# One product of 512 columns for the two that share a weight's high part, in the last swiglu of a two-layer hybrid block

## The chip, the core and the metric

The kernel runs on one core of one Trainium2 chip. The metric is the device time of one execution in microseconds; the profiled execution also has a span, from its first to its last instruction. The engines are TensorE (PE; PEld is its weight load), VectorE (DVE), ScalarE (ACT), GpSimd (POOL) and SyncE (SP, which issues the DMAs).

## The reference

256 tokens of x and 256 of a context, 1024 features wide, go through two layers. Each layer is a swiglu, a mixer (a short convolution in the first, attention in the second) and another swiglu, each behind an RMS norm that is modulated by a condition. The context is dropped after the attention, so the last swiglu works on 256 tokens alone:

```python
def _swiglu(h, w13, w2):
    gte, up = jnp.split(h @ w13, 2, axis=-1)
    return (jax.nn.silu(gte) * up) @ w2
...
lat = lat + 0.5 * mod[:, 2, 2] * _swiglu(_modulate(lat, norm_g[i, 2], mod[:, 2, 0], mod[:, 2, 1]), ffn_w13[i, 1], ffn_w2[i, 1])
```

w13 is 1024 x 5632 (gate and up, 2816 each), w2 is 2816 x 1024, all in float32.

## The kernel before

Features lie on the 128 partitions, tokens in the columns: x is a tile of 8 feature blocks (KT = 8) x 512 columns (S = 256 tokens of x, then 256 of the context; T2 = 512).

**Three matmuls per product.** Every float32 operand is split into a high part that TensorE's fp32r format holds and the low part that is left (`split`, L97: ACT writes the high part, L98, and DVE subtracts it from the source, L99). A product of a weight w and a moving operand m is then wh*mh + wh*ml + wl*mh, three matmuls into the same PSUM region: `mm3`, L122 to L124. The weight is the stationary operand (128 x 128), and each matmul loads its own.

**The last swiglu** is `ffn(1, 1, hn, S, ...)` at the end of the kernel, with tot = S = 256 columns. Its 22 blocks of 128 hidden features are done in three parts ("thirds") of 8, 7 and 7:

- *Gate part.* For each block, `load_w` fetches 1 MB of w13 over SP's queue and splits it in two halves of 1024 columns (up first, then gate; four buffers for the halves of each part). `w13_mm` runs over the 8 k of the input features and, for each, makes the gate product into PSUM tile pg and the up product into pu. `w13_post` applies Silu (ACT, L535, to sg), multiplies by up (DVE, L537, to gm) and splits the result into gh and gl, two tiles of a pool with 8 buffers each.
- *Second product* (`project`). For each of 8 output tiles m, w2's weights are split (896 or 1024 columns), products over the third's 7 or 8 blocks go into PSUM tile py, and `finish` (L453, DVE) adds gate * py to x. The first two output tiles are begun with all blocks but the last, then both get the last block; the other tiles follow one by one. In the last third, each finished tile goes out with a DMA (L1143).

The input h of this swiglu is made by `norm_k` for each k: DVE scales x (t, L264), ACT adds the bias and writes the high part hh (L274), DVE writes the low part hl (L275). They lie in tiles of class `Plain`: with w = S each tile of 1024 columns holds the high, or the low, parts of four k.

PSUM has six buffers of 512 columns for pg, pu and py. The order of instructions on each engine is made by a planner that goes by estimated times and priorities; only the start of the kernel has PE's order written out by hand.

The output projection of the attention ahead of it (`by_pairs("wo")`) also calls `project` with 256 columns, with operands in two separate slices (aos).

Of the kernel before, what the change touches and what calls it, by code (L numbers as in the profile page):

```python
# [16 lines left out]
P = 128  # L17
# [24 lines left out]
def hybrid_kernel(ctx: ExitStack, tc: tile.TileContext, a: dict, out: bass.AP):  # L42
# [54 lines left out]
    def split(hi, lo, src):  # L97
        nc.scalar.activation(out=hi, in_=src, func=AF.Copy)  # L98
        nc.vector.tensor_tensor(out=lo, in0=src, in1=hi.bitcast(F32), op=ALU.subtract)  # L99
# [17 lines left out]

    def mm3(ps, w, m, first, last, more=False):
        wh, wl = w
        mh, ml = m  # L120
        kw = {"skip_group_check": True} if more else {}
        nc.tensor.matmul(ps, wh, mh, start=first, stop=False, **kw)  # L122
        nc.tensor.matmul(ps, wh, ml, start=False, stop=False, **kw)  # L123
        nc.tensor.matmul(ps, wl, mh, start=False, stop=last, **kw)  # L124
# [155 lines left out]
    def hot(s, dt=F32R):  # L280
        return hop.tile([P, 1024], dt, name=nm(s), tag="hop")

    class Plain:


        def __init__(self, w=T2):
            self.w, self.n = w, 1024 // w
            self.t = [(hot("hh"), hot("hl")) for _ in range(KT // self.n)]

        def at(self, k, c0, c1):  # L290
            o = (k % self.n) * self.w
            return tuple(t[:, o + c0 : o + c1] for t in self.t[k // self.n])

    def pick(h, k, c0, c1):
        return h.at(k, c0, c1)
# [92 lines left out]
    def new_pair(s):  # L388

        return (  # L390
            gp.tile([P, T2], F32R, name=nm(s + "h"), tag="gh"),
            gp.tile([P, T2], F32R, name=nm(s + "l"), tag="gl"),
        )
# [51 lines left out]

        return tail

    def finish(m, ps, c0, c1, gate, tail):
        g = gate()
        for s in range(2):  # L450
            if c0 <= s * S < c1:
                o = s * S - c0
                nc.vector.scalar_tensor_tensor(  # L453
                    out=x[:, m, s * S : s * S + S],
                    in0=ps[:, o : o + S],
                    scalar=g[:, m, s : s + 1],
                    in1=x[:, m, s * S : s * S + S],
                    op0=ALU.mult,
                    op1=ALU.add,
                )  # L460
        if tail:
            tail(m, c0, c1)
# [6 lines left out]
    def project(ws, src, nk, gate, tail, tot, late, ev, between=()):  # L469

        def products(ps, w, ks, c0, c1):
            for k in ks:
                mm3(ps[:, : c1 - c0], w(k), src(k, c0, c1), k == 0, k == nk - 1)

        nf = 3 if between else 2  # L480
        ahead = {}

        def get(m):
            for i in range(m, min(m + 3, KT)):
                if i not in ahead:
                    ahead[i] = ws(i)
            return ahead[m]

        w2 = [get(m) for m in range(nf)]
        p2 = [psum("py") for _ in range(nf)]  # L490
        cut = nk - 2 if between else nk - 1
        for i in range(nf):
            products(p2[i], w2[i], range(cut), 0, tot)
            if i < len(between):
                between[i]()
        if between:
            for i in range(nf):
                products(p2[i], w2[i], (nk - 2,), 0, tot)
        for i in range(nf):
            products(p2[i], w2[i], (nk - 1,), 0, tot)  # L500
            finish(i, p2[i], 0, tot, gate, tail)
            tick(ev)

        for m in range(nf, KT - late):
            if tail and tot == S and m == KT - 2:
                ready()
            w = get(m)
            ps = psum("py")
            products(ps, w, range(nk), 0, tot)
            finish(m, ps, 0, tot, gate, tail)  # L510
            tick(ev)
        if late:

            wl = [get(m) for m in (6, 7)]
            if tail:
                ready()
            for s in range(2):
                for i in range(2):
                    ps = psum("py")
                    products(ps, wl[i], range(nk // 2), s * S, s * S + S)  # L520
                    flush(1)
                    products(ps, wl[i], range(nk // 2, nk), s * S, s * S + S)
                    finish(6 + i, ps, s * S, s * S + S, gate, tail)


    def w13_mm(pp, w, h, ks, c0, c1):
        for k in ks:
            mv = pick(h, k, c0, c1)
            for i in range(2):
                mm3(pp[i][:, c0:c1], w((1 - i) * 1024 + k * P), mv, k == 0, k == KT - 1)  # L530

    def w13_post(pp, g, c0, c1):
        n = c1 - c0
        sg = tp.tile([P, T2], F32, name=nm("sg"), tag="sg", bufs=3)
        nc.scalar.activation(out=sg[:, :n], in_=pp[0][:, :n], func=AF.Silu)  # L535
        gm = tp.tile([P, T2], F32, name=nm("gm"), tag="gm", bufs=3)
        nc.vector.tensor_tensor(out=gm[:, :n], in0=sg[:, :n], in1=pp[1][:, :n], op=ALU.mult)  # L537
        split(g[0][:, c0:c1], g[1][:, c0:c1], gm[:, :n])

    class Pair:  # L540

# [76 lines left out]
    def ffn(l, b, h, tot, gate, tail, gs=(), ev=1.5):  # L618
        gs = list(gs)
        i0 = 0  # L620
        for t, n in enumerate(THIRDS):
            between = ()
            if tot == T2:
                heads = []
                if t == 0 and not gs:

                    w = [load_w(a["w13"][l, b, 0])]
                    gs = [new_pair("g") for _ in range(2)]
                    pp = [(psum("pg"), psum("pu")) for _ in range(2)]
                    w13_mm(pp[0], w[0], h, range(KT), 0, S)  # L630
                    flush()
                    w.append(load_w(a["w13"][l, b, 1]))
                    w13_mm(pp[1], w[1], h, range(KT), 0, S)
                    h.sums(0)
                    w13_mm(pp[0], w[0], h, range(KT), S, T2)
                    w13_post(pp[0], gs[0], 0, T2)
                    heads.append(Pair(a["w13"][l, b, 2], h))
                    h.sums(1)
                    heads[0].sums(0)
                    w13_mm(pp[1], w[1], h, range(KT), S, T2)  # L640
                    w13_post(pp[1], gs[1], 0, T2)
                    heads[0].head()
                    h.sums(2)
                    heads[0].sums(1)
                prev = None
                for i in range(len(gs), n):
                    if t == 0 and not heads and i in AS_IS[l, b]:
                        w = load_w(a["w13"][l, b, i])
                        pp = psum("pg"), psum("pu")
                        if prev:  # L650
                            prev.seven()
                        w13_mm(pp, w, h, range(4), 0, T2)
                        if prev:
                            gs.append(new_pair("g"))
                            prev.four(gs[-1])
                            prev = None
                        w13_mm(pp, w, h, range(4, KT), 0, T2)
                        gs.append(new_pair("g"))
                        w13_post(pp, gs[-1], 0, T2)
                        tick(5)  # L660
                        continue
                    if heads:
                        pr = heads.pop(0)
                    else:
                        pr = Pair(a["w13"][l, b, i0 + i], h)
                        pr.sums(0)
                        pr.sums(1)
                        pr.head()
                    pr.five()
                    if prev:  # L670
                        prev.seven()
                    pr.six()
                    if prev:
                        gs.append(new_pair("g"))
                        prev.four(gs[-1])
                    prev = pr

                def last():
                    gs.append(new_pair("g"))
                    prev.four(gs[-1])  # L680

                between = (prev.seven, last) if prev else ()
            else:
                for i in range(n):
                    w = load_w(a["w13"][l, b, i0 + i])
                    gs.append(new_pair("g"))
                    pp = psum("pg"), psum("pu")
                    w13_mm(pp, w, h, range(KT), 0, tot)
                    w13_post(pp, gs[i], 0, tot)
                    tick(1)  # L690
            i0 += n
            box = {}
# [1 line left out]
            def ws2(m):  # L694
# [9 lines left out]
            cur = gs  # L704
            end = t == len(THIRDS) - 1
            project(
                ws2, lambda k, c0, c1: (cur[k][0][:, c0:c1], cur[k][1][:, c0:c1]), n,
                gate, tail if end else None, tot, 2 if end and tot == T2 else 0, ev, between,
            )
            gs = []  # L710
# [423 lines left out]
    mix(HEADS - 1, pts.pop(HEADS - 1))  # L1134


    hn = Plain(S)
    project(
        by_pairs("wo"), lambda k, c0, c1: aos[k], KT, lazy_gate(1, 1), tail_norm(1, 2, hn), S, 0, 0,
    )  # L1140
# [84 lines left out]
```

## Time and profile before

| | us |
|---|---|
| median of three runs | 1597.02 (1593.21 to 1598.21) |
| the profiled execution | 1595.53 |
| its span | 1593.7 |
| of that, the last swiglu: first matmul to last | 1398.37 to 1590.21 |
| gate part of its thirds (8, 7, 7 blocks) | 47.8, 40.2, 40.2 |
| second product of its thirds | 22.9, 20.0, 20.0 |
| mean granted TensorE clock | 0.993 |

The parts of the thirds are given from the start of their first matmul to the start of their last. In the last swiglu TensorE runs 22 x 16 x 3 = 1056 matmuls for the gate part and 22 x 8 x 3 = 528 for the second product, all of 256 columns.

How to read the lines: a row of the timeline gives start, length, engine, line of the kernel, operation, output <- inputs and shapes, a count if several were merged, and in brackets the idle time before it and what ended it. The length of a matmul holds its way through the array and overlaps with the next one; the distance of two starts is what one costs in a row.

### The profile page before, as it was taken

The numbers are of one execution on the slowest core, as the hardware profiler recorded it, in microseconds if no ns is written. First come the engines' busy times: TensorE is split into PE (matmuls) and PEld (weight loads), VectorE is DVE, ScalarE is ACT, GpSimd is POOL, SyncE is SP. The second block draws the span as 40 slices with busy tenths as digits, with TensorE's granted clock in tenths as the row PEclk, the third lists the DMA queues.
The fourth block names the chain that finished last, engine by engine and source line by source line (L and its number), as shares of the span: only waits on it lengthen the run. The fifth ranks groups of instructions, "written<-read, shape, count | busy, mean of one in ns | idle before, by whom it ended". The sixth has DMA issues, their size and how long they took to land.

```text
span 1593.7 us, 25820 instructions
## 1 busy us (share of the span) xinstructions
PE 1568.8 (98%) x10666; PEld 1449.7 (91%) x10666; DVE 1303.3 (82%) x1984; ACT 721.1 (45%) x1103; POOL 29.4 (2%) x20
## 2 busy tenths in 40 slices
PE   8999999999999999999999999999999998899999
PEld 7688998999888899989899899899899897899999
DVE  5998888979999879798798879898797789876554
ACT  6522452544322356335345365335255455644443
POOL 0000000000000000000000000000000005200000
PEclk9999999999999999999999999999999999999999
DMA  9465324334565522452342513443433554556452
GB/s 359 181 238 207 110 99 153 133 102 176 177 219 195 175 68 93 148 170 100 129 156 96 180 56 107 158 136 99 169 118 120 208 186 151 200 185 220 166 200 102
DMA packets 39575, 248.79 MB, mean 156 GB/s; under 512 B 5409, under 2 KB 7201, under 8 KB 14625
## 3 DMA queue, kind: packets, MB, share of 16 engines
q1 hardware_dynamic: 36864, 245.38, 43.9%
q10 hardware_dynamic: 2592, 1.76, 0.4%
q8 instruction: 83, 1.36, 0.3%
q14 instruction: 36, 0.29, 0.1%
HBM read 244.77 MB, written 1.05 MB: 154 GB/s over the span
## 4 chain that ended last, share of the span: by engine, by line
PE 92%; DVE 4%; ACT 2%; DMA 1%; issue 0%; POOL 0%; ACTq 0%; DVEq 0%; POOLq 0%
PE py L123 10%; PE py L122 10%; PE py L124 10%; PE p L124 7%; PE p L123 7%; PE p L122 6%; PE q L122 5%; PE q L124 5%; PE q L123 5%; PE pg L122 2%; PE pg L124 2%; PE pg L123 2%; PE pu L124 2%; PE pu L123 2%; PE pu L122 2%; PE pv L122 1%
## 5 line engine op out<-in xcount | busy, mean ns | idle before, releaser
L98 ACT ACTIVATE wh<-wr 128x1024 fp32r<-128x1024 f32 (+2 forms) x276 | 276.4, 1014 | 388.0 <-PE py L123 140.7
L99 DVE TENSOR_TENSOR wl<-wr,wh 128x1024 fp32r<-128x1024 f32 (+2 forms) x276 | 319.9, 1166 | 88.2 <-ACT wh L98 87.9
L142 DVE CUSTOM_DVE_ANT_0 junk<-wr,scbc,modb 128x1024 bf16<-128x1024 f32 x224 | 286.9, 1281 | 31.8 <-DMA wr<-in_modT 29.0
L122 PE MATMUL py<-gh,wh 128*128 128x512 f32 (+1 forms) x746 | 263.3, 353 | 0.0
L123 PE MATMUL py<-gl,wh 128*128 128x512 f32 (+1 forms) x746 | 263.0, 353 | 0.0
L124 PE MATMUL py<-gh,wl 128*128 128x512 f32 (+1 forms) x746 | 262.7, 352 | 0.0
L99 DVE TENSOR_TENSOR wl<-ws,wh 128x1024 fp32r<-128x1024 f32 x108 | 131.6, 1223 | 34.1 <-ACT wh L98 34.0
L124 PEld LDWEIGHTS py<-gh,wl 128*128 128x128 f32 x746 | 141.1, 189 | 19.0
L122 PEld LDWEIGHTS py<-gh,wh 128*128 128x128 f32 x746 | 141.2, 189 | 18.6
L123 PEld LDWEIGHTS py<-gl,wh 128*128 128x128 f32 x746 | 141.2, 189 | 18.1
L98 ACT ACTIVATE wh<-ws 128x1024 fp32r<-128x1024 f32 x108 | 113.9, 1058 | 71.3 <-PE p L123 44.5
L124 PE MATMUL p<-th,wl 128*128 128x256 f32 x432 | 122.3, 283 | 0.0
L123 PE MATMUL p<-tl,wh 128*128 128x256 f32 x432 | 122.2, 283 | 0.0
L122 PE MATMUL p<-th,wh 128*128 128x256 f32 x432 | 122.2, 283 | 0.0
L453 DVE SCALAR_TENSOR_TENSOR x<-py,G,x 128x256 f32<-128x256 f32 x168 | 73.9, 477 | 23.1 <-PE py L124 23.1
L122 PE MATMUL q<-bh,wh 128*128 128x256 f32 x320 | 90.6, 283 | 0.0
L123 PE MATMUL q<-bl,wh 128*128 128x256 f32 x320 | 90.6, 283 | 0.0
L124 PE MATMUL q<-bh,wl 128*128 128x256 f32 x320 | 90.6, 283 | 0.0
L122 PEld LDWEIGHTS p<-th,wh 128*128 128x128 f32 x432 | 82.9, 192 | 0.3
L123 PEld LDWEIGHTS p<-tl,wh 128*128 128x128 f32 x432 | 82.9, 192 | 0.3
L124 PEld LDWEIGHTS p<-th,wl 128*128 128x128 f32 x432 | 82.9, 192 | 0.0
L124 PE MATMUL pg<-hh,wl 128*128 128x256 f32 (+1 forms) x240 | 75.5, 315 | 2.8 <-DVE wl L99 2.7
(236 smaller groups left out, 4045.2 us busy)
## 6 DMA issues: line engine op xcount, KB each, us to landing
wr<-in_w SPq DMA_DIRECT2D x88, 1024.0 KB, 4.9
wr<-in_modT SPq DMA_DIRECT2D x64, 1024.0 KB, 5.0
wr<-in_w2b SPq DMA_DIRECT2D x32, 896.0 KB, 4.6
wr<-in_w2a SPq DMA_DIRECT2D x16, 1024.0 KB, 4.9
pm<-in_mod SPq DMA_DIRECT2D x16, 512.0 KB, 10.0
wr<-in_cw_cx SPq DMA_DIRECT2D x8, 1024.0 KB, 4.9
wr<-in_cw_b SPq DMA_DIRECT2D x4, 1024.0 KB, 5.0
wr<-in_cw_out SPq DMA_DIRECT2D x4, 1024.0 KB, 4.9
```

The source lines that it names most:

```text
L98: nc.scalar.activation(out=hi, in_=src, func=AF.Copy)
L99: nc.vector.tensor_tensor(out=lo, in0=src, in1=hi.bitcast(F32), op=ALU.subtract)
L122: nc.tensor.matmul(ps, wh, mh, start=first, stop=False, **kw)
L123: nc.tensor.matmul(ps, wh, ml, start=False, stop=False, **kw)
L124: nc.tensor.matmul(ps, wl, mh, start=False, stop=last, **kw)
L142: nc.vector.tensor_tensor_reduce(out=junk, in0=raw[:, j * D : j * D + D], in1=scbc[:, v, :], scale=1.0, scalar=modb[:, l, col : col + 1], ...
L453: nc.vector.scalar_tensor_tensor(out=x[:, m, s * S : s * S + S], in0=ps[:, o : o + S], scalar=g[:, m, s : s + 1], in1=x[:, m, s * S : s * ...
```

## The change

In the last swiglu the high and low part of an operand now lie side by side in one tile. `Beside` holds h that way (two k per tile, each 256 columns high and 256 low), and one tile gx of 512 columns takes the place of gh and gl. An operand that comes as three views (high, low, both) is multiplied with two matmuls: the weight's high part meets both in one of 512 columns, and the weight's low part meets the high part in one of 256 columns, into the first half of the PSUM tile. So the PSUM tile holds wh*mh + wl*mh in the first half and wh*ml in the second, and the halves are added when they are read.

For gate and up this is `beside_post`: ACT copies the second half out of PSUM, DVE adds the first to it, for both, and Silu, product and split follow as before on 256 columns. In the second product `finish` adds gate * half to x once for each half. The last output tile (m = 7) of each third keeps the three matmuls of 256 columns.

```diff
     def mm3(ps, w, m, first, last, more=False):
         wh, wl = w
+        kw = {"skip_group_check": True} if more else {}
+        if len(m) == 3:
+
+            nc.tensor.matmul(ps, wh, m[2], start=first, stop=False, **kw)
+            nc.tensor.matmul(ps[:, :S], wl, m[0], start=False, stop=last, **kw)
+            return
         mh, ml = m
-        kw = {"skip_group_check": True} if more else {}
...
+    class Beside:
+
+
+        def __init__(self):
+            self.t = [hot("hx") for _ in range(KT // 2)]
+
+        def both(self, k):
+            o = (k % 2) * T2
+            return beside(self.t[k // 2][:, o : o + T2])
+
+        def at(self, k, c0, c1):
+            return self.both(k)[:2]
+
+    def beside(t):
+        return t[:, :S], t[:, S:], t
...
-    def finish(m, ps, c0, c1, gate, tail):
+    def finish(m, ps, c0, c1, gate, tail, wide=False):
         g = gate()
         for s in range(2):
-            if c0 <= s * S < c1:
-                o = s * S - c0
+            for o in [s * S - c0] if not wide else range(0, T2 if s == 0 else 0, S):
+                if not c0 <= s * S < c1:
+                    continue
                 nc.vector.scalar_tensor_tensor(
...
-        def products(ps, w, ks, c0, c1):
+        def products(ps, w, ks, c0, c1, wide=True):
             for k in ks:
-                mm3(ps[:, : c1 - c0], w(k), src(k, c0, c1), k == 0, k == nk - 1)
+                m = src(k, c0, c1)
+                if not wide:
+                    m = m[:2]
+                n = T2 if len(m) == 3 else c1 - c0
+                mm3(ps[:, :n], w(k), m, k == 0, k == nk - 1)
...
-            products(ps, w, range(nk), 0, tot)
-            finish(m, ps, 0, tot, gate, tail)
+            wide = len(src(0, 0, tot)) == 3 and m < KT - 1
+            products(ps, w, range(nk), 0, tot, wide)
+            finish(m, ps, 0, tot, gate, tail, wide)
...
+    def beside_post(pp, g):
+
+        sg = tp.tile([P, T2], F32, name=nm("sg"), tag="sg", bufs=3)
+        gm = tp.tile([P, T2], F32, name=nm("gm"), tag="gm", bufs=3)
+        for o, p in ((sg, pp[0]), (gm, pp[1])):
+            nc.scalar.copy(o[:, S:], p[:, S:])
+            nc.vector.tensor_tensor(out=o[:, :S], in0=p[:, :S], in1=o[:, S:], op=ALU.add)
+        nc.scalar.activation(out=sg[:, :S], in_=sg[:, :S], func=AF.Silu)
+        nc.vector.tensor_tensor(out=gm[:, :S], in0=sg[:, :S], in1=gm[:, :S], op=ALU.mult)
+        split(g[0], g[1], gm[:, :S])
...
-                    gs.append(new_pair("g"))
+                    gs.append(beside(gp.tile([P, T2], F32R, name=nm("gx"), tag="gh")))
                     pp = psum("pg"), psum("pu")
-                    w13_mm(pp, w, h, range(KT), 0, tot)
-                    w13_post(pp, gs[i], 0, tot)
+                    for k in range(KT):
+                        for j in range(2):
+                            mm3(pp[j], w((1 - j) * 1024 + k * P), h.both(k), k == 0, k == KT - 1)
+                    beside_post(pp, gs[i])
...
-    hn = Plain(S)
+    hn = Beside()
```

More of the change, by code (lines that the diff above doesn't have):

```diff
@@ L283, in hybrid_kernel, with __init__ @@
     class Plain:
-        def __init__(self, w=T2):
-            self.w, self.n = w, 1024 // w
-            self.t = [(hot("hh"), hot("hl")) for _ in range(KT // self.n)]
+        def __init__(self):
+            self.t = [(hot("hh"), hot("hl")) for _ in range(KT // 2)]
         def at(self, k, c0, c1):
-            o = (k % self.n) * self.w
-            return tuple(t[:, o + c0 : o + c1] for t in self.t[k // self.n])
+            o = (k % 2) * T2
+            return tuple(t[:, o + c0 : o + c1] for t in self.t[k // 2])
+    class Beside:
+        def __init__(self):
+            self.t = [hot("hx") for _ in range(KT // 2)]
+        def both(self, k):
+            o = (k % 2) * T2
+            return beside(self.t[k // 2][:, o : o + T2])
[3 more added lines that the diff above has]
+        return t[:, :S], t[:, S:], t
     def pick(h, k, c0, c1):
@@ L500, in project @@
             products(p2[i], w2[i], (nk - 1,), 0, tot)
-            finish(i, p2[i], 0, tot, gate, tail)
+            finish(i, p2[i], 0, tot, gate, tail, len(src(0, 0, tot)) == 3)
             tick(ev)
@@ L706, in ffn @@
             project(
-                ws2, lambda k, c0, c1: (cur[k][0][:, c0:c1], cur[k][1][:, c0:c1]), n,
+                ws2,
+                (lambda k, c0, c1: cur[k]) if tot == S
+                else lambda k, c0, c1: (cur[k][0][:, c0:c1], cur[k][1][:, c0:c1]), n,
                 gate, tail if end else None, tot, 2 if end and tot == T2 else 0, ev, between,
```

## The prediction

> **What bounds the kernel now.** I read the page first (busy time by engine, chain that ended last), then the windows of the last swiglu, then its matmuls in order of time, then the places where work on other engines could come on the path.
>
> ```profile
> PE 1568.8 (98%) x10666; PEld 1449.7 (91%) x10666; DVE 1303.3 (82%) x1984; ACT 721.1 (45%) x1103; POOL 29.4 (2%) x20
> ...
> PE 92%; DVE 4%; ACT 2%; DMA 1%; issue 0%; POOL 0%; ACTq 0%; DVEq 0%; POOLq 0%
> ```
>
> TensorE is busy all the time, and 92% of the chain is its matmuls. The windows cut the last swiglu into gate part and second product of each third (columns: window, its length, busy time and instructions of PE, PEld, DVE, ACT, POOL, clock, DMA share, GB/s):
>
> ```profile
> 1398.30:1446.30 48.00, 47.92 (x384) 47.72 (x385) 32.85 (x53) 23.39 (x38) 0.00 (x0) 0.96 0.61 218
> 1446.30:1469.30 23.00, 23.00 (x194) 23.00 (x193) 14.72 (x18) 9.81 (x11) 0.00 (x0) 1.00 0.60 204
> 1469.30:1509.60 40.30, 40.30 (x338) 40.30 (x338) 19.61 (x26) 17.17 (x26) 0.00 (x0) 1.00 0.48 164
> 1509.60:1529.80 20.20, 20.20 (x171) 20.20 (x170) 13.92 (x18) 9.23 (x11) 0.00 (x0) 1.00 0.61 205
> ```
>
> No window has a hole in PE; DVE is at 49 to 69%, ACT at 43 to 49%, DMA at about 0.6. So a matmul saved here is time saved, as long as nothing else becomes late. The second gate part is 7 tiles x 48 = 336 matmuls of 256 columns; the first starts at 1469.38 and the last at 1509.58, 335 pitches in 40.20 us: **0.1200 us** each. Where 512 columns are used (conv stage, first start 411.10, last 557.31, 645 pitches) it is **0.2267 us**. One product of 512 is cheaper than two of 256: 0.2400 - 0.2267 = 0.0133 us. A mix of both lengths stands in the second layer's first swiglu (start, length, engine, line):
>
> ```profile
> 1239.37 0.39 PE L124 MATMUL py<-gh,wl 128*128 128x512 f32 x1
> 1239.60 0.28 PE L122 MATMUL p<-th,w4h 128*128 128x256 f32 x1
> 1239.71 0.28 PE L123 MATMUL p<-tl,w4h 128*128 128x256 f32 x1
> ...
> 1240.91 0.28 PE L124 MATMUL p<-th,w4l 128*128 128x256 f32 x1
> 1241.03 0.40 PE L122 MATMUL py<-gh,wh 128*128 128x512 f32 x1
> 1241.26 0.40 PE L123 MATMUL py<-gl,wh 128*128 128x512 f32 x1
> ```
>
> A 256 after a 512 starts 0.23 us later, a 512 after a 256 starts 0.12 us later: the pitch belongs to the matmul that runs, and a change of length costs nothing.
>
> **The change, part by part.**
>
> *Merged products.* Gate part: 22 tiles x 8 k x 2 (gate, up) = 352 products. Second product: 22 k x 7 output tiles = 154; the eighth tile (m = 7) keeps three matmuls in every third. Each of the 506 goes from 3 x 0.1200 = 0.3600 to 0.2267 + 0.1200 = 0.3467 us: 506 x 0.0133 = **-6.73**. In the first 3.4 us of the stage (1398.37 to 1401.8) the 256 columns have a pitch of 0.213, which is 256 columns at half of the rate and no fixed part; some 5 products there save nothing: **+0.07**. The output projection keeps its three matmuls.
>
> The Trainium skill, "TensorE: Matmul & The Clock Gate", section "Back-to-back issue gap", puts the fixed part of a warm matmul at 2.5 ns beside N/2.4. By it a merge would be worth 2.5 ns and all 506 about 1.3 us, an estimate from that page. The trace says 13.3 ns, at 256 and at 512 columns alike, and the sum goes by the trace.
>
> *Start of the stage.* The wide product needs both parts of h, the first product of before only the high one.
>
> ```profile
> 1397.81 0.91 ACT L274 ACTIVATE hh<-t,mod 128x256 fp32r<-128x256 f32 x2 [2.13 <-DVE t L264]
> 1398.37 0.58 PE L122 MATMUL pg<-hh,wh 128*128 128x256 f32 x1 [1.11 <-ACT hh L274]
> 1398.47 0.48 DVE L275 SCALAR_TENSOR_TENSOR hl<-t,mod,hh 128x256 fp32r<-128x256 f32 x1
> ```
>
> PE starts 0.06 after the first hh; it will start 0.04 or so after the first hl, at 1398.99: **+0.62**. Later k are not late: the hl come at 0.42 each, a k costs PE 2 x (0.427 + 0.213) = 1.28 us while slow (512 columns at twice 0.213) and 2 x 0.3467 = 0.69 after, and the last two hl (ready 1404.45 and 1404.88) meet PE at about 1404.7.
>
> *Longer way from gate product to g.* For each of 22 tiles: two copies on ACT (0.36 each, row L602 of 256 columns out of PSUM) and two adds on DVE (0.41, as gm of L537; 0.36 between starts) come ahead of Silu. Inside a third nothing waits for g. What could wait is the next weights: DVE's second split of a tile ends at 1501.73 (start 1500.51, 1.22 long) and its matmuls start at 1503.84, 2.11 us to spare. A tile then lasts 5.55 in place of 5.74, and two adds take 0.72: 1.20 us are left, so 0. At the end of a third the second product needs the last g:
>
> ```profile
> 1569.94 0.95 ACT L98 ACTIVATE wh<-wr 128x896 fp32r<-128x896 f32 x1 [2.90 <-PE pg L123]
> 1570.80 0.37 ACT L535 ACTIVATE sg<-pg 128x256 f32<-128x256 f32 x1
> ...
> 1572.39 0.42 ACT L98 ACTIVATE gh<-gm 128x256 fp32r<-128x256 f32 x1 [0.38 <-DVE gm L537]
> ```
>
> ```profile
> 1570.93 1.09 DVE L99 TENSOR_TENSOR wl<-wr,wh 128x896 fp32r<-128x896 f32 x1 [3.00 <-ACT wh L98]
> 1571.94 0.41 DVE L537 TENSOR_TENSOR gm<-sg,pu 128x256 f32<-128x256 f32 x1
> 1572.27 1.09 DVE L99 TENSOR_TENSOR wl<-wr,wh 128x896 fp32r<-128x896 f32 x1
> 1573.27 0.42 DVE L99 TENSOR_TENSOR gl<-gm,gh 128x256 fp32r<-128x256 f32 x1
> ```
>
> PE begins the second product at 1570.17 and covers 2 output tiles x 6 k before it needs the last g: 2 x 6 x 0.36 = 4.32, to 1574.49; gl ends at 1573.69. Afterwards the cover is 4.16. Walking the queues with the same splits in them (wl, add, add, wl, then gm, gh, gl, since gm waits for Silu while wl is ready) gl ends about 4.8 after the start: 0.65 late. In the third with 8 tiles the cover is 14 x 0.3467 = 4.85 against about 5.05: 0.2 late. Together 0.65 + 0.65 + 0.2 = 1.5. With gm ahead of the second split, or with PE given products of the third output tile meanwhile, it is 0. The upper bound is all new work in series, 2 copies 0.72 + 2 adds 0.82 + Silu behind them 0.47 + gh no longer under a split 0.5 = 2.5: late by 1.9, 1.9 and 1.5, 5.3 in all. Between 0 and the walk I take **+0.75**.
>
> *finish.* 21 more x += gate * ps on DVE. A pair takes 0.88 where one takes 0.48 (row L453 x2 at 1575.06); in the second product DVE then works 1.09 + 0.88 = 1.97 of 2.43 us per tile, and the second one lies under the 0.95 of ACT's next weight split, which the DVE split awaits anyway: 0. Uncovered it would be 21 x 0.40 = 8.4. The last tile is as before, so the tail after the last matmul (0.48 and the output) is too.
>
> *Storage.* hx takes four buffers as hh and hl did, gx one where there were two; no DMA is added or moved, and a weight MB per 5.55 us asks for 4% more than now, at a share of 0.6. 0.
>
> **Sum:** -6.73 + 0.07 + 0.62 + 0.75 = **-5.29 us**. The profiled execution took 1595.53 (span 1593.7 and 1.8 around it): **1590.2**. Against the median 1597.02 of the three runs it would be 1591.7; those runs spread over 5 us, and the profiled one lies inside them. 0.3% of the time is 4.8 us.
>
> **Rivals.**
>
> *The g chain stalls every third.* For it: only 0.8 us are spare now, and two engines with strict order take part. Against it: PE can be given other products. With the upper bound 5.3 in place of 0.75: 1595.53 - 6.04 + 5.3 = 1594.8, no measurable change.
>
> *The fixed part isn't saved.* If the cost went by columns alone, nothing is gained and 0.62 + 0.75 is paid: 1596.9. Against it stands 0.2267 in place of 0.24 in every stage with 512 columns, and the mix above. If a part of it is saved, the time lies between 1596.9 and 1590.2. By the page of the Trainium skill named above it would be about 1595.6, with 2.5 ns a product; the trace speaks against it.
>
> *Slower: DVE holds the weights back.* If its order puts the whole chain of a tile (two copies and adds 2 x 0.77, Silu 0.37, gm 0.41, gh 0.42, gl 0.42: 3.2 us) ahead of the second weight split, that split comes 2.9 later than now (0.24 lies between the two splits today), against 1.92 to spare. PE then waits 1.0 us in each of the 19 tiles that another gate tile follows in its third: 1590.2 + 19 = 1609. It decides from 1.92 us of delay on, and is slower than before from 0.5 us per tile. For it: DVE and ACT already take turns on each tile. Against it: a ready split is let ahead of gm in every tile of the trace (wl, gm, wl, gl).
>
> *It doesn't do what it says* where a product falls back to three matmuls; by the code only m = 7 does, and that is in the sum.
>
> **How the numbers follow.** Forecast 0.64, its own range 1588 to 1592.5 (stalls of 0 to 2, and some 1 us of run to run); as its middle is just over the bound of 4.8, 0.54 of it is faster by over 0.3% and 0.10 within. Stalled thirds 0.16 and no fixed part, or a small one, 0.10: both within 0.3%. DVE holding weights back 0.10: slower. So faster 0.54, same 0.36, slower 0.10. The range goes from 1587.5 (no stall, a run 1 us under this one) to 1596.0, which takes in the stalled thirds and the small fixed part.
>
> **What would show it.** Matmuls from 10666 to 10160; in the last swiglu pitches of 0.227 and 0.120 in turn, a gate tile in 5.55 us and an output tile in 2.43 (2.77 in the first third); the first matmul of the stage about 0.6 us later, behind hl; PE idle of under 1 us at the three starts of the second product, put down to the split of g. It is wrong if a 256 after a 512 of the same bank has another pitch, if weight splits show up ahead of idle PE in every tile, or if the work ahead of 1398 is ordered otherwise.

## The result, and the profile after

The changed kernel takes 1592.12 us (median of 20 runs, 1588.40 to 1597.26), the kernel before 1596.58 (20 runs, 1592.36 to 1598.21). The ratio is 0.9976 with a 95% interval of 0.9969 to 0.9983: 3.8 us faster, 2.7 to 4.9. The forecast was 5.3 us, to 1590.2, counted from a profiled execution 1 us below the median of the kernel before.

The profiled execution of the changed kernel is one of the slower ones: its span is 1595.4 us, longer than the 1593.7 of the one before. It comes to the last swiglu late: the output projection's last matmul starts at 1397.47, before at 1392.83, with the same number of matmuls ahead of it. The clock is the likely reason: in the stretches 20 to 40, 70 to 85 and 1335 to 1350 us the mean granted clock was 0.83, 0.77 and 0.89, against 0.93, 0.89 and 1.00 before, which by an estimate (difference times length) is some 5 us of full clock. So the two traces are compared from that matmul on. To the start of the last matmul of all, it is 1590.21 - 1392.83 = 197.38 us before and 1591.92 - 1397.47 = 194.45 after, 2.93 less.

The page of the changed kernel, busy time and the shares of the chain that ended last:

```profile
PE 1568.9 (98%) x10160; PEld 1425.1 (89%) x10160; DVE 1327.1 (83%) x2049; ACT 735.7 (46%) x1147; POOL 28.4 (2%) x20
...
PE 92%; DVE 4%; DMA 2%; ACT 2%; issue 0%; POOL 0%; ACTq 0%; DVEq 0%; POOLq 0%
```

506 matmuls fewer, 65 instructions more on DVE and 44 on ACT, and PE still bounds the kernel.

The windows of the changed kernel from its first gate product on (window, length, busy time of PE, PEld, DVE, ACT, POOL, granted clock, DMA share, GB/s; x counts instructions), then the first window of the kernel before:

```profile
1403.44:1408.57 5.13, 5.13 (x16) 4.37 (x17) 5.13 (x13) 2.32 (x6) 0.00 (x0) 0.50 0.25 107
1408.57:1450.99 42.42, 42.42 (x242) 36.87 (x241) 31.69 (x53) 24.85 (x44) 0.00 (x0) 1.00 0.65 226
1473.50:1513.08 39.58, 39.58 (x227) 34.35 (x225) 24.14 (x38) 21.40 (x38) 0.00 (x0) 1.00 0.47 167
1513.08:1532.78 19.70, 19.70 (x122) 17.41 (x121) 17.02 (x27) 9.85 (x13) 0.00 (x0) 1.00 0.63 215
```

```profile
1398.37:1401.83 3.46, 3.46 (x16) 3.46 (x17) 3.46 (x10) 2.05 (x5) 0.00 (x0) 0.50 0.49 206
```

The clock column first: the stage starts at half clock in both, for 3.46 us before and 5.13 after. Over the 13 profiles of this case it is between 2.8 and 5.9 us, with early and late starts alike. Half of it is lost, so the changed kernel's profile lost 0.84 us more to it; without that it gained 2.93 + 0.84 = 3.77, as the ratio has it.

The parts of the thirds, from the start of the first matmul to the start of the last:

| us | before | after | difference | forecast by merged products alone |
|---|---|---|---|---|
| gate part, 8 blocks (half clock in it) | 47.84 | 47.43 | -0.41 | -1.70 |
| second product, 8 blocks | 22.92 | 22.40 | -0.52 | -0.74 |
| gate part, 7 blocks, twice | 40.20 | 39.45 | -0.75 each | -1.49 each |
| second product, 7 blocks, twice | 20.04 | 19.57 | -0.47 each | -0.65 each |

The second products gained nearly what was forecast. The gate parts of 7 blocks gained half; that of 8 gained 0.41 + 0.84 = 1.25 of 1.70, once the longer half clock is taken off. Matmuls of a gate part in order of time (start, length):

```profile
1480.22 0.40 PE L123 MATMUL pu<-hx,wh 128*128 128x512 f32 x1
1480.46 0.28 PE L124 MATMUL pu<-hx,wl 128*128 128x256 f32 x1
1480.58 0.40 PE L123 MATMUL pg<-hx,wh 128*128 128x512 f32 x1
1480.82 0.28 PE L124 MATMUL pg<-hx,wl 128*128 128x256 f32 x1
1480.93 0.40 PE L123 MATMUL pu<-hx,wh 128*128 128x512 f32 x1
```

and those of a later output tile of the second product:

```profile
1522.99 0.40 PE L123 MATMUL py<-gx,wh 128*128 128x512 f32 x1
1523.22 0.28 PE L124 MATMUL py<-gx,wl 128*128 128x256 f32 x1
1523.34 0.39 PE L123 MATMUL py<-gx,wh 128*128 128x512 f32 x1
1523.57 0.27 PE L124 MATMUL py<-gx,wl 128*128 128x256 f32 x1
1523.68 0.40 PE L123 MATMUL py<-gx,wh 128*128 128x512 f32 x1
```

Read the starts of the 512s. In the gate part two products take 1480.93 - 1480.22 = 0.71 us, in the second product 1523.68 - 1522.99 = 0.69. Over whole tiles it is **0.3533 us** a product in the gate part (5.65 us for 16) and **0.3467** in the later output tiles. So against 0.3600 for three matmuls the merge saves 0.0067 us here and 0.0133 there, with the same two instructions. In the mean of the second gate part (108 starts each) the next matmul starts 0.237 us after a 512 and 0.117 after a 256, where rows of one length have 0.2267 and 0.1200: what got longer is the 512.

The start and the ends of the thirds went as reckoned. The start in the changed kernel:

```profile
1402.91 1.27 DVE L280 SCALAR_TENSOR_TENSOR hx<-t,mod,hx 128x256 fp32r<-128x256 f32 x3
...
1403.44 0.80 PE L123 MATMUL pg<-hx,wh 128*128 128x512 f32 x1 [2.05 <-DVE hx L280]
```

PE now waits for DVE's low part, where before it waited for ACT's high part. The end of the second third on DVE:

```profile
1513.85 1.09 DVE L99 TENSOR_TENSOR wl<-wr,wh 128x896 fp32r<-128x896 f32 x1 [1.65 <-ACT wh L98]
...
1514.86 0.42 DVE L572 TENSOR_TENSOR sg<-pg,sg 128x256 f32<-128x256 f32 x1
...
1515.19 0.41 DVE L572 TENSOR_TENSOR gm<-pu,gm 128x256 f32<-128x256 f32 x1
...
1515.52 1.08 DVE L99 TENSOR_TENSOR wl<-wr,wh 128x896 fp32r<-128x896 f32 x1
...
1516.52 0.42 DVE L574 TENSOR_TENSOR gm<-sg,gm 128x256 f32<-128x256 f32 x1
...
1517.42 0.42 DVE L99 TENSOR_TENSOR gx<-gm,gx 128x256 fp32r<-128x256 f32 x1 [0.48 <-ACT gx L98]
```

This is the walk of the prediction (wl, add, add, wl, gm, gl): the last g is whole at 1517.84, 4.76 us after the second product began at 1513.08. The waits of the weight loads in the whole swiglu (us in total, times, longest):

```profile
PEld py L123 <- DVE gx L99: 0.5, 3, 0.2
```

PE lost 0.2 at each of the three ends, since it was given one product and a half of the third output tile meanwhile. No weight load waits for a weight split.

### The profile page after: what moved, and what is told of

The parts are those of the page before. It is cut to its first block, busy times and chain, and to the rows that moved or that the text cites. A ratio compares the mean times of both kernels' runs of the same rounds, so it can differ in the third digit from the quotient of the medians.

```text
span 1595.4 us, 24933 instructions
## 1 busy us (share of the span) xinstructions
PE 1568.9 (98%) x10160; PEld 1425.1 (89%) x10160; DVE 1327.1 (83%) x2049; ACT 735.7 (46%) x1147; POOL 28.4 (2%) x20
## 4 chain that ended last, share of the span: by engine, by line
PE 92%; DVE 4%; DMA 2%; ACT 2%; issue 0%; POOL 0%; ACTq 0%; DVEq 0%; POOLq 0%
PE py L127 9%; PE py L128 9%; PE py L129 9%; PE p L129 6%; PE p L128 6%; PE p L127 6%; PE q L127 5%; PE q L129 5%; PE q L128 5%; PE pg L123 3%; PE pu L123 3%; PE py L123 2%; PE pg L124 1%; PE pu L124 1%; PE pg L129 1%; PE pg L127 1%
## 5 line engine op out<-in xcount | busy, mean ns | idle before, releaser
L127 PE MATMUL py<-gh,wh 128*128 128x512 f32 (+1 forms) x570 | 213.5, 375 | 0.0
L128 PE MATMUL py<-gl,wh 128*128 128x512 f32 (+1 forms) x570 | 213.2, 374 | 0.0
L129 PE MATMUL py<-gh,wl 128*128 128x512 f32 (+1 forms) x570 | 212.9, 373 | 0.0
L129 PEld LDWEIGHTS py<-gh,wl 128*128 128x128 f32 x570 | 107.3, 188 | 19.1
L127 PEld LDWEIGHTS py<-gh,wh 128*128 128x128 f32 x570 | 107.4, 188 | 18.3
L128 PEld LDWEIGHTS py<-gl,wh 128*128 128x128 f32 x570 | 107.4, 188 | 18.2
L474 DVE SCALAR_TENSOR_TENSOR x<-py,G,x 128x256 f32<-128x256 f32 x189 | 83.3, 477 | 16.5 <-PE py L129 9.7
L123 PE MATMUL pg<-hx,wh 128*128 128x512 f32 x176 | 71.2, 405 | 2.1 <-DVE hx L280 2.1
```

Of the source, the lines that this page charges most:

```text
L123: nc.tensor.matmul(ps, wh, m[2], start=first, stop=False, **kw)
L474: nc.vector.scalar_tensor_tensor(out=x[:, m, s * S : s * S + S], in0=ps[:, o : o + S], scalar=g[:, m, s : s + 1], in1=x[:, m, s * S : s * ...
```

## The experiments

What was open: why a merged product costs 0.3533 in one place and 0.3467 in another, and whether the start and the halves of the change are worth what the trace says. The first four runs separate the parts and change the order of the matmuls.

**One half of the change alone.** e1_gate_only gives the second product its three matmuls back:

```diff
-                (lambda k, c0, c1: cur[k]) if tot == S
+                (lambda k, c0, c1: cur[k][:2]) if tot == S
```

> Theory A (a merged product costs 0.3533 us instead of 0.3467 wherever the length of the moving operand changes with every matmul, so the gate part gains 0.0067 a product): gate parts as in the changed kernel (39.45 us in the second and third third against 40.2 before), second products as before (20.04); about 352 x 0.0067 = 2.3 gained, some 0.5 to 1 of it lost at the start of the stage: 1.3 to 1.9 us faster than before. Rival B (the longer pitch is a state that TensorE falls into after a stretch without a wait and leaves with a wait): the same for this kernel. If the prediction's size were right (0.0133 a product) it would be 4.0 us.

Measured: ratio 0.9990 (0.9979 to 1.0001), 1.6 us as expected, but by the interval only just not told from no change. The gate thirds of 7 blocks are 39.45, as in the changed kernel; the second products take 20.27 instead of 20.04, because here too the last g is some 0.23 late (PE goes on at 1511.56, the low part of g ends at 1511.50).

e2_second_only does the gate part in three matmuls of 256 with the old `w13_post`:

```diff
-                            mm3(pp[j], w((1 - j) * 1024 + k * P), h.both(k), k == 0, k == KT - 1)
-                    beside_post(pp, gs[i])
+                            mm3(pp[j][:, :S], w((1 - j) * 1024 + k * P), h.both(k)[:2], k == 0, k == KT - 1)
+                    w13_post(pp, gs[i], 0, tot)
```

> Gate part and start of the stage as before (first product behind the first high part; 40.2 us in the second third), second products with the merged matmul. Theory A: the output tiles show the longer pitch in all tiles, 0.3533 a product, 49 x 0.0067 = 0.33 us gained per third, 1.0 us in all. Rival B: the tiles behind a wait for the last g have 0.3467, the first two may have 0.3533: 0.5 per third, 1.5 us in all. The halves of e1 and this one should add up to the 3.8 us of the whole change.

Measured: ratio 0.9995 (0.9985 to 1.0004), not told from no change. The start is 5.33 us behind the output projection, gate thirds 40.20, second products 19.71, with 0.3533 a product in all merged tiles. Without a wait for g, the second product has the long pitch too, and gains 0.33 a third. That fits theory A and rival B alike, as PE had not waited there. So it isn't the alternation between two PSUM banks that makes it, for py is one bank. The two halves add up to 2.4 us of the 3.8; the intervals are too wide to say that anything is missing. Nor need the halves add up: the changed kernel and e1 pay the waits for g, e2 doesn't.

**The order of the lengths.** e3_two_two does the gate part as gate 512, up 512, gate 256, up 256 (`mmw` and `mmn` are the two matmuls of a merged product):

```diff
                     for k in range(KT):
                         for j in range(2):
-                            mm3(pp[j], w((1 - j) * 1024 + k * P), h.both(k), k == 0, k == KT - 1)
+                            mmw(pp[j], w((1 - j) * 1024 + k * P), h.both(k), k == 0)
+                        for j in range(2):
+                            mmn(pp[j], w((1 - j) * 1024 + k * P), h.both(k), k == KT - 1)
```

> Gate part in the order gate 512, up 512, gate 256, up 256 for each k; second product as in the changed kernel. Theory A: half as many changes of length, half of the extra 6.7 ns: 0.3500 a product, a gate tile of 5.60 us (5.64 in the changed kernel), third of 7 tiles 39.2. Rival B: order is of no account, 5.64 and 39.45.

Measured: ratio 0.9965 (0.9952 to 0.9979), 5.6 us. The gate part of e3:

```profile
1476.81 0.40 PE L133 MATMUL pg<-hx,wh 128*128 128x512 f32 x1
1477.04 0.40 PE L133 MATMUL pu<-hx,wh 128*128 128x512 f32 x1
1477.28 0.28 PE L136 MATMUL pg<-hx,wl 128*128 128x256 f32 x1
1477.40 0.27 PE L136 MATMUL pu<-hx,wl 128*128 128x256 f32 x1
1477.51 0.40 PE L133 MATMUL pg<-hx,wh 128*128 128x512 f32 x1
```

Two products take 1477.51 - 1476.81 = 0.70; a tile of 16 is 5.57 (0.3483 each) and a third of 7 tiles 38.89, where the changed kernel has 39.45. That is a larger gain than theory A expected (39.2). The same matmuls in another order are 0.56 us a third cheaper, so rival B as put for this run, that order is of no account, falls: order changes the loss. A change between wh and wl is not enough for it: rows of one length change in the same way, at 0.1200 and 0.2267.

e4_eight_eight does eight 512s and then eight 256s of one tile:

```diff
-                    for k in range(KT):
-                        for j in range(2):
-                            mm3(pp[j], w((1 - j) * 1024 + k * P), h.both(k), k == 0, k == KT - 1)
+                    for j in range(2):
+                        for k in range(KT):
+                            mmw(pp[j], w((1 - j) * 1024 + k * P), h.both(k), k == 0)
+                        for k in range(KT):
+                            mmn(pp[j], w((1 - j) * 1024 + k * P), h.both(k), k == KT - 1)
```

> Gate part with eight matmuls of 512 for the gate, then its eight of 256, then the same for up; second product as in the changed kernel. Theory A: four changes of length in a tile instead of 32: 0.3467 a product plus little, a gate tile of 5.55 to 5.57 us, third of 7 tiles 38.9, 1.7 us faster over the stage than the changed kernel. Rival B: 39.45 as it was. In the first tile all eight k are needed before the first 256, so its start may lose up to 1.5 us unless the second tile fills in.

Measured: ratio 0.9965 (0.9950 to 0.9979), thirds of 7 tiles 38.99. In the trace the eights are merged to rows:

```profile
1466.73 2.00 PE L133 MATMUL pg<-hx,wh 128*128 128x512 f32 x8
1468.58 1.12 PE L136 MATMUL pg<-hx,wl 128*128 128x256 f32 x8
1469.53 2.00 PE L133 MATMUL pu<-hx,wh 128*128 128x512 f32 x8
...
1472.32 2.00 PE L133 MATMUL pg<-hx,wh 128*128 128x512 f32 x8
```

A tile is 1472.32 - 1466.73 = 5.59, 0.3494 a product: with four changes of length in place of 32 it is not better than the twos. So theory A, a fixed price for each change of length, falls as well. Within the rows, a 512 takes (1468.58 - 1466.73) / 8 = 0.231 us and a 256 (1469.53 - 1468.58) / 8 = 0.119: the 512 is above its 0.2267 even in a row of eight. e8_four_four takes fours:

```diff
-                    for k in range(KT):
-                        for j in range(2):
-                            mm3(pp[j], w((1 - j) * 1024 + k * P), h.both(k), k == 0, k == KT - 1)
+                    for q in range(0, KT, 2):
+                        for k in (q, q + 1):
+                            for j in range(2):
+                                mmw(pp[j], w((1 - j) * 1024 + k * P), h.both(k), k == 0)
+                        for k in (q, q + 1):
+                            for j in range(2):
+                                mmn(pp[j], w((1 - j) * 1024 + k * P), h.both(k), k == KT - 1)
```

> Gate part with four matmuls of 512 (gate and up of two k) and then four of 256. If the loss goes with the number of changes of length, the third of 7 tiles takes 38.85 us or a little less (39.45 in turn, 38.89 in twos); the eight in a row of e4 had 0.3500 a product, above the twos, and if that holds for long rows of one bank's matmuls, it is between, 38.9 to 39.2.

Measured (a single run, 1595.64 us, which alone tells nothing of the time): a third of 7 tiles 39.17, within the expected 38.9 to 39.2, a tile 5.61, 0.3508 a product. In turn 0.3533, fours 0.3508, eights 0.3494, twos 0.3483: it doesn't fall with the number of changes.

**Is it the next weights, loaded under a matmul that is too short?** Three kernels, each run once, are the changed kernel with another length of the gate part's second matmul (here 272 columns):

```diff
-                            mm3(pp[j], w((1 - j) * 1024 + k * P), h.both(k), k == 0, k == KT - 1)
+                            wj, hk = w((1 - j) * 1024 + k * P), h.both(k)
+                            nc.tensor.matmul(pp[j], wj[0], hk[2], start=k == 0, stop=False)
+                            nc.tensor.matmul(pp[j][:, :272], wj[1], hk[2][:, :272], start=False, stop=k == KT - 1)
```

> The changed kernel, the gate part's second matmul on 272 columns (the first 16 of the low part too, which adds their wl*ml). 16 columns are 6.7 ns at full clock, from the 0.1067 us between 512 and 256. Theory L (the next weights, those of the 512, are loaded while the short matmul runs and are not ready at its end; this sets the longer pitch): a product stays at 0.353 us, a third of 7 tiles at 39.45. Theory C (pitch is columns plus a constant): 0.360, third 40.2.

> The same with 288 columns, 13.3 ns more. Theory L: 0.353 to 0.360 (some of it comes out of the hidden load), third 39.5 to 40.2. Theory C: 0.3667, third 40.9.

> The same with 224 columns: the weight's low part is left out for the last 32 tokens of the gate part. Theory L: nothing is gained, 0.353, third 39.45. Theory C: 0.340, third 38.0.

Measured, in the traces: thirds of 7 tiles of 38.35 (224 columns), 39.45 (256), 40.21 (272) and 40.56 (288). 16 columns more cost their full price, 0.0067 a product, and 32 columns fewer save 0.0099 of their 0.0133: theory L falls, the weight load doesn't set the pitch by itself. Theory C is right at 272 and off at the ends. What is left above the columns (0.4167 ns each) is 37 ns a product at 224, 33 at 256 and 272, 30 at 288, and 27 in the later output tiles: it moves by some ns with the length, and with the order too (28 in twos, 29 in eights, 31 in fours). Where this comes from wasn't found.

e11 took 1600.15 us, where the kernel before took 1595.15 beside it. It shows, in its first third, the rival that was feared for the change. Its waits from 1400 to 1432:

```profile
DVE junk L147 <- DMA wr<-in_modT: 7.0, 2, 3.7
...
PEld pg L729 <- DVE wl L99: 3.6, 1, 3.6
```

The planner put a job of the modulation (junk), whose data were on their way, ahead of a weight split in DVE's order; DVE stood still for it and PE for the split; over the whole swiglu its weight loads wait 5.3 us for splits. In the changed kernel they wait for none.

**Twos in both parts, and the start.** e5_pairs_both adds to e3 the same order in the second product, two k at a time:

```diff
+            if wide and len(src(0, c0, c1)) == 3:
+                for i in range(0, len(ks), 2):
+                    for k in ks[i : i + 2]:
+                        mmw(ps, w(k), src(k, c0, c1), k == 0)
+                    for k in ks[i : i + 2]:
+                        mmn(ps, w(k), src(k, c0, c1), k == nk - 1)
+                return
```

> The order of e3 in the gate part, and in the second product two k at a time: 512, 512, 256, 256 (the odd k alone). If the order sets the pitch as in e3 (0.3483 us a product, where 512 and 256 in turn cost 0.3533), a second product of 7 blocks lasts 19.5 to 19.6 us instead of 19.80 in e3, gate thirds 38.89 as there, 0.7 us less than e3 in all. If only the two PSUM banks of the gate part made the difference, the second products stay at 19.8.

Measured: ratio 0.9972 (0.9958 to 0.9985); gate thirds 38.90, second products 19.68, a gain of 0.12 on e3's 19.80 where 0.2 to 0.3 was expected, with 0.2 of it spent waiting for g. By the ratio it isn't told from e3.

e7_first3 and e6_pairs_first3 let the first gate tile start behind the high part, in the changed kernel and in e5:

```diff
+                    if t == 0 and i == 0:
+                        w13_mm(pp, w, h, range(KT), 0, S)
+                        w13_post(pp, gs[i], 0, S)
+                    else:
```

> The changed kernel with only its first gate tile in three matmuls of 256. Start 5.4 instead of 6.1 us behind the output projection, gate parts of the second and third third 39.45 as in the changed kernel; 0.5 us faster than the changed kernel if the start term holds, so a ratio to before near 0.9973.

> e5 with the first gate tile in three matmuls of 256, which can start behind the first high part of h. If the start term of the prediction holds, PE's first matmul comes 5.4 us after the last of the output projection instead of 6.1, and the tile itself loses 0.1 to 0.2 to its longer products at full clock: 0.5 us faster than e5. If the start is set by something else (the clock is at half rate there), no difference.

Measured: PE starts 5.32 and 5.33 us behind the output projection's last matmul, and 5.96 to 6.18 in the nine profiles with a wide first product, so the place of the start is right. But the ratios are 0.9974 (0.9963 to 0.9986) against 0.9976 of the changed kernel, and 0.9965 (0.9953 to 0.9978) against 0.9972 of e5: no gain that can be told. The intervals reach more than 1 us each way, so a gain of 0.6 us or less could not show. In e6's own profile PE starts 0.64 earlier than in e5 behind the output projection, but the half clock ends 11.2 us behind it in both, so the time won runs at half clock; the first third's gate part took 47.54 in place of 46.94, which gives the start back. e7's profile also has the long pitch in two of its second products (22.64 and 19.82 us, in the changed kernel 22.40 and 19.57), which would hide such a gain.

## Why the prediction was right, and where it was off

**What bounds it.** Right: PE at 98% and no new hole but 0.5 us.

**The sum as measured.** With 0.84 us for the clock taken off, the traces give: gate parts -(1.25 + 0.75 + 0.75) = -2.75, second products -1.96 without their waits, waits for g +0.5, start +0.43 (5.97 us behind the output projection, before 5.54): -3.8, as the ratio has it. The forecast was -5.29.

**Merged products, -6.73.** The mechanism was right, the size is the step that was off: -4.7 measured. The second products have most of it: 1.46 us measured plus 0.5 of waits, against 2.05. The gate parts have 2.75 of 4.68; those of 7 blocks have half, 0.75 against 1.49. The prediction named the sign itself, that a 256 after a 512 of the same bank has another pitch, and it came: 0.117 instead of 0.120 behind a 512 of 0.237, a gate tile of 5.65 us and not 5.55. The prediction took 0.2267 and 0.1200 from rows where one length follows itself, and held up the mixed spot of the second layer as proof that a change of length is free. That spot has one change after twelve matmuls of one length; here the length changes with every matmul. Starts rounded to 0.01 us cannot show 6.7 ns at a single change. e3 shows that the order matters: twos bring 0.56 of the missing 0.74 us a third back. Why is open, and order is not all of it, as one order has both pitches in one trace.

**The rule of the Trainium skill** ("TensorE: Matmul & The Clock Gate", section "Back-to-back issue gap", 2.5 ns beside N/2.4 for a warm matmul) would have made the merges worth 1.3 us, an estimate from that page. The traces have 4.7 for them, and the whole change gained 3.8, with 2.7 as the lower end. The 13.3 ns of the kernel before stand for rows of one length.

**Start, +0.62.** The place and the size are right, like for like: in the four profiles where the clock was already halved 3 us behind the output projection (0.50), PE starts 5.54 us behind it with a narrow and 6.18 with a wide first product, in the others 5.33 and 5.97: 0.64 later. Its worth may be smaller than written, since PE runs at half clock there; e7 and e6 found no gain from taking it away, but could not have told 0.6 us from nothing. The 0.07 for products at half clock came from a stretch of 3.4 us; the stretch itself varies by 3 us from profile to profile.

**End of the thirds, +0.75.** 0.5 in total. gl came 4.76 us after the start, 4.8 was reckoned. The planner's fill with products of the third output tile, which the prediction named, is what kept it from 1.5. That 0.75 came near is chance: it was taken between 0 and 1.5 without a reason for the middle.

**finish and storage, 0.** No wait in the trace names the extra adds on x.

**Rivals.** The stalled thirds didn't come. DVE holding back the weights didn't come either, but e11 shows that a change of the same kind can bring it about by the planner's order alone. "The fixed part isn't saved" was nearest to the truth in the gate part, where half of it isn't; its argument against, the mixed spot, was the weak point.

**Luck and chances.** The prediction gave 0.54 to a gain of over 0.3% and 0.36 to one within it; the measured 0.24% is within. Its range went up to 1596.0, beyond the profiled execution of the kernel before (1595.53), so that the time fell into it says little. And that the second products had nearly their full size was luck: it hung on the short pitch after the waits for g, which e2, without those waits, did not have (0.33 us a third in place of 0.65), nor e3 with them.

## What to carry to other kernels

One matmul of 512 columns in place of two of 256 that share a weight saves the fixed part of a matmul, here 13.3 ns at best and 6.7 ns where 512 and 256 columns alternate; in the gate part, putting them in twos (two long, two short) brought 0.56 us a third back. Price a mixed stream from a mixed stream, over whole tiles: single starts in a trace are too coarse for a difference of some ns that occurs hundreds of times. The best orders tried, twos or eights in the gate part, are at 0.9965 of the kernel before (0.9952 to 0.9979 for the twos); against the changed kernel's 0.9976 the intervals overlap.

## What was not expected of the hardware

The sum of the two pitches has more than one value for the same instructions in the same order: 0.3533 and 0.3467 in one trace. In the changed kernel the short one came after a stretch in which PE had waited (the start of the stage, the last g), and it went over to the long one without a cause in the trace, at about 1417; in e7 the second third's second product took 19.82 us and the last third's 19.57. But not every wait brought it: e3 waits for g too and has 19.80 in both. And it came without one: the second product of e8's second third has the short pitch from its start at 1511.52 (twelve products to 1515.68, 0.3467 each), behind a gate part without a wait, and the long one after its wait for g. And the half clock at the start of the stage lasted 2.8 to 5.9 us, up to 1.5 us of time. Not all of that is the kernel's doing: e1 and the changed kernel run the same matmuls in the same order to the end of the first gate part, with 2.9 us in one and 5.1 in the other.
